# Neighbourhood attention as one stream, its transposes set one by one between score matmuls

## The chip, the cores and the metric

The kernel runs on one core of one Trainium2 chip. The metric is device time in microseconds (us), the median of a few executions. Before the change it is 2613.26 us (three runs, 2611.22 to 2614.13).

A core has five engines that run beside each other: TensorE (PE in the profile; its weight loads are shown as PEld), VectorE (DVE), ScalarE (ACT), GpSimd (POOL) and SyncE (SP). Here SP does nothing but issue the transfers between HBM and the on-chip memory. Each engine works off its own list of instructions in order; semaphores tie the lists together.

## The reference, cut to what matters

One encoder layer on two sequences, 1024 "prompt" and 256 "sample" tokens, model width 2048, all in float32. It normalises, projects to 9232 columns, runs two head groups beside each other, projects back and normalises again.

```
hn = rmsnorm(x, norm_w);  proj = hn @ w_in
att = neighbourhood_attention(q, k, v, rpb) * silu(gate)      # 8 heads of 128
mem = rmsnorm(bidirectional_mlstm(...)) * sigmoid(o) * silu(z) # 4 heads of 256
y   = rmsnorm(x + concat(att, mem) @ w_out)
```

The tokens lie on a grid 64 wide. In the attention, a query sees a window of 8 rows by 16 columns of keys (4 rows in the sample), with a learned bias for each relative place:

```
s = einsum(q_row, k_window) * scale + bias;  p = softmax(s);  out = einsum(p, v_window)
```

## The kernel before, in words

**Precision.** Every float32 product is made of three matmuls: each operand is split into a rounded high part and a low rest (`split`, lines 149 to 155: ACT writes the high part, line 151, DVE the rest, line 152), and high x high, high x low and low x high are added in PSUM. Transposes are matmuls against the identity, on the unsplit data.

**PSUM.** There are eight banks of 512 columns (`bank`, line 66): three with the tag "pr", five with the tag "a". A tile of a tag takes a bank once the instructions on an earlier tile of the tag have finished.

**Stages, in order of time.**

1. To about 1100 us: the projection of the first 768 tokens, in pairs of 128 columns (`pair_a`, line 316), as a seven-product Strassen scheme. Each of four rounds `r` loads a weight tile and makes seven products of six matmuls each (line 188), 384 columns wide, into seven banks: three "pr", four "a". What is left to do for a pair (`finish_a`, line 284) is a generator which the next pair pulls on between its products: `next(bg, None)` after the products 5, 4 and 2 of the rounds 0 to 2 (line 382). For the v columns (eight pairs), `finish_a` transposes: two transposes (line 310) to a bank, a copy by ACT (line 312), a store, six times over.
2. From about 1100 to 2110 us: the other 512 tokens' projections (line 499; v at line 580), the mLSTM and the attention. In four rounds `i`, the projections of a round are followed by `run` (line 1134, called at line 1161), which interleaves two streams with high priority: the mLSTM's units of head `i`, and the attention of the heads `2i` and `2i + 1`.
3. From about 2110 us: the output product (line 1302) and the last normalisation.

**The attention.** Per head there are five jobs: the sample (`na_sample`) and four column blocks of the prompt (`na_prompt`, `block`). A job loads v, and for each of its two halves makes the scores (three matmuls, line 617, 384 or 256 columns) in a bank, loads the bias, and makes the softmax (`na_softmax`): DVE adds the bias and takes the maximum (line 622), ACT takes the exponential with its sum (line 625), DVE inverts the sum (line 626), ACT scales (line 627). Then `na_transpose` turns each half: three transposes (two in the sample; line 634) into one bank, from which ACT writes the high part (line 636) and DVE the rest (line 637) to a tile `pt`, of which there is one buffer. Last comes the product with v (twelve matmuls in a block, line 743), and its way out. Queries and keys of a head (`nqk`) have one buffer too, and are loaded and split ahead of its blocks.

In program order, a block's stages are: all of its scores and softmaxes; a `yield`; the split of v and its transposes, in runs of three and three; a `yield`; the product. Units of a stream overlap, since `run` takes a new unit at each pass.

**What sets the order on the engines.** The kernel is recorded in program order and then put in order by a list scheduler, which takes for each engine, by priority (program order, with the streams of `run` first), what its model holds ready. It may mix projections into the attention, and does. The order on each engine is fixed when the program is built.

Of the kernel before, what the change touches and what calls it, by code (L numbers as in the profile page):

```python
# [1 line left out]

# [6 lines left out]
F32 = mybir.dt.float32  # L9
F32R = mybir.dt.float32r  # L10
AF = mybir.ActivationFunctionType
ALU = mybir.AluOpType

P = 128
D = 2048
KT = D // P
TS = 256
TP = 1024
# [20 lines left out]
def kernel(  # L39
# [244 lines left out]
    def finish_a(n1, Cn):  # L284
        nm = f"A{n1}"
        for j in range(2):
            if n1 >= NCH:
                break
            if QK0 <= n1 < OT0:
                ct = n1 - QK0 + j  # L290
                DM.dma_start(qb[ct], Cn[j][:, GA - 4 :])
                cv = pc(f"{nm}cv{j}")
                yield from conv_taps(cv, Cn[j], ct, GA - 2, 2)
                DM.dma_start(cD[ct][:, : GA - 2], cv[:, : GA - 2])
            else:
                if OT0 <= n1 < ZT0:
                    S.activation(Cn[j], Cn[j], AF.Tanh, scale=0.5)
                elif n1 >= GT0:
                    th = pc(f"{nm}th{j}")
                    S.activation(th, Cn[j], AF.Tanh, scale=0.5)  # L300
                    V.scalar_tensor_tensor(Cn[j], th, 1.0, Cn[j], op0=ALU.add, op1=ALU.mult)
                DM.dma_start(pT[n1 + j][:, 0:GA], Cn[j])
            yield
        if n1 >= NCH:
            yield
            yield
            for tt in range(GA // P):
                b = bank("a", f"{nm}v{tt}")
                for j in range(2):
                    PE.transpose(b[:, j * P : (j + 1) * P], Cn[j][:, tt * P : (tt + 1) * P], ident)  # L310
                o = wa.tile([P, 256], F32, tag="vo", name=f"{nm}vo{tt}", bufs=2)
                S.copy(o, b[:, :256])
                DM.dma_start(vD[(n1 - NCH) // 2][tt * P : (tt + 1) * P, :], o)
                yield

    def pair_a(n1, bg=iter(()), hook=None):
        nm = f"A{n1}"
        tags = ("pr", "pr", "pr", "a", "a", "a", "a")
        order = (1, 5, 6, 4, 7, 2, 3)
# [29 lines left out]
        for r in range(4):  # L349
# [12 lines left out]
            for i in order:  # L362
# [81 lines left out]

    bg = iter(())
    for i, n1 in enumerate(order):
        bg = pair_a(n1, bg, second_pools if i == len(order) - 1 else None)
# [166 lines left out]
    def na_softmax(nm, qs, ks, nkeys, h, boff):  # L614
        b = bank("a", f"{nm}s")
        for i, (a_, b_) in enumerate(((0, 0), (0, 1), (1, 0))):
            PE.matmul(b[:, :nkeys], qs(a_), ks(b_), start=i == 0, stop=i == 2)
        bt = na_tile("nbt", [P, NAK], f"{nm}bt", 2)[:, :nkeys]
        DM.dma_start(bt, rpb_tab[h, :, boff : boff + nkeys])
        st = na_tile("nst", [P, NAK], f"{nm}st", 3)[:, :nkeys]  # L620
        sm = na_tile("sm", [P, 4], f"{nm}sm", 4)
        V.tensor_tensor_reduce(
            st, b[:, :nkeys], bt, -1.0, 3.0e38, ALU.add, ALU.min, sm[:, 0:1],
        )
        S.activation(st, st, AF.Exp, bias=sm[:, 0:1], scale=-1.0, accum_out=sm[:, 2:3])
        V.reciprocal(sm[:, 3:4], sm[:, 2:3])
        S.mul(st, st, sm[:, 3:4])
        return st

    def na_transpose(nm, st, order, dst):  # L630
        b = bank("a", f"{nm}t")
        n = len(order)
        for i, c in enumerate(order):
            PE.transpose(b[:, i * P : (i + 1) * P], st[:, c * P : (c + 1) * P], ident)
        bv = b[:, : n * P].rearrange("p (k q) -> p k q", q=P)
        S.copy(dst[0], bv)
        V.tensor_tensor(dst[1], bv, f(dst[0]), op=ALU.subtract)

    def na_sample(h):
        nm = f"nas{h}"  # L640
        qk = na_tile("nqk", [P, 4, TP], f"{nm}qk", 1, F32R)[:, :, :TS]
        for i, src in enumerate((pT[QT0 + h], pT[KT0 + h])):
            raw = na_tile("nraw", [P, 512], f"{nm}r{i}", 2)[:, :TS]
            DM.dma_start(raw, src[:, TP:])
            split(qk[:, 2 * i], qk[:, 2 * i + 1], raw)
        yield
        v = na_tile("nv", [P, 2, 512], f"{nm}v", 2, F32R)
        raw = na_tile("nraw", [P, 512], f"{nm}rv", 2)[:, :TS]
        DM.dma_start(
            raw.rearrange("p (t c) -> p t c", c=P),  # L650
            vD[h // 2][TP:, (h % 2) * P : (h % 2 + 1) * P].rearrange("(t p) c -> p t c", p=P),
        )
        split(v[:, 0, :TS], v[:, 1, :TS], raw)
        st = [
            na_softmax(
                f"{nm}_{t}", lambda a_: qk[:, a_, t * P : (t + 1) * P],
                lambda b_: qk[:, 2 + b_, :], TS, h, BIAS_S + t * TS,
            )
            for t in range(2)
        ]  # L660
        yield
        pt = na_tile("npt", [P, 2, 768], f"{nm}pt", 1, F32R)
        for t in range(2):
            na_transpose(
                f"{nm}_{t}", st[t], (0, 1),
                [
                    pt[:, z, :512].rearrange("p (s q) -> p s q", s=2)[:, :, t * P : (t + 1) * P]
                    for z in range(2)
                ],
            )  # L670
        yield
        b = bank("a", f"{nm}o")
        for c in range(2):
            for i, (a_, b_) in enumerate(((0, 0), (0, 1), (1, 0))):
                PE.matmul(
                    b[:, :TS], v[:, a_, c * P : (c + 1) * P], pt[:, b_, c * TS : (c + 1) * TS],
                    start=c == 0 and i == 0, stop=c == 1 and i == 2,
                )
        o = na_tile("nst", [P, NAK], f"{nm}ot", 3)[:, :TS]
        S.copy(o, b[:, :TS])  # L680
        DM.dma_start(mixT[h][:, TP:], o)
        yield

    def na_prompt(h):
        nm = f"nap{h}"
        hd = {}

        def setup():
# [17 lines left out]
            yield  # L706

        def block(c4):
            q, k = hd["q"], hd["k"]
            n2 = f"{nm}_{c4}"  # L710
            kc = KC0[c4]
            kv = [x_.rearrange("p (r c) -> p r c", c=64) for x_ in k]
            v = na_tile("nv", [P, 2, 512], f"{n2}v", 2, F32R)
            raw = na_tile("nraw", [P, 512], f"{n2}vr", 2)
# [3 lines left out]
            st = [  # L718
                na_softmax(
                    f"{n2}_{rh}",  # L720
                    lambda a_: q[a_][:, rh * 512 + c4 * P : rh * 512 + (c4 + 1) * P],
                    lambda b_: kv[b_][:, 4 * rh : 4 * rh + 12, kc : kc + 32],
                    NAK, h, (BKIND[c4] * 2 + rh) * NAK,
                )
                for rh in range(2)
            ]
            yield
            split(v[:, 0], v[:, 1], raw)
            pt = na_tile("npt", [P, 2, 768], f"{n2}pt", 1, F32R)
            for rh in range(2):  # L730
                na_transpose(
                    f"{n2}_{rh}", st[rh], ((1, 2, 0), (0, 1, 2))[rh],
                    [
                        pt[:, z].rearrange("p (s r q) -> p s r q", r=2, q=P)[:, :, rh, :]
                        for z in range(2)
                    ],
                )
            yield
            b = bank("a", f"{n2}o")
# [7 lines left out]
            ov = hd["o"].rearrange("p (r c) -> p r c", c=64)  # L747
# [5 lines left out]
            )  # L753
            S.copy(ov[:, ng:, cs], bv[:, ng:])
            if c4 == 3:
                DM.dma_start(mixT[h][:, :TP], hd["o"])
            yield

        yield setup()
        for c4 in range(4):  # L760
            yield block(c4)

    def ml_tris():
        t = mid("tris")
# [383 lines left out]
    for i in range(ML_H):  # L1148
# [319 lines left out]
```

## Time and profile before

| | |
|---|---|
| median of three runs | 2613.26 us (2611.22 to 2614.13) |
| the profiled execution | 2613.54 us |
| its span, first to last instruction | 2611.8 us |
| instructions | 42439 |
| matmuls, transposes among them | 14470 |
| VectorE busy | 1930.9 us |
| ScalarE busy | 1311.1 us |
| bytes moved | 389.10 MB |

The profile is of one execution on the chip. A row of a group names line, engine, operation, the tiles written and read, and shapes; "x12" counts its instructions. PE rows carry the matmuls, PEld rows the loads of their weights, which run beside matmuls. In the order of time, a row gives the start, the length from the first start to the last end, and the group; neighbours of one kind are one row. The ends of matmuls are modelled, so matmuls that follow each other overlap in the record. A wait row reads: who waited, for whom, us in total, times, the longest.

The costliest groups (busy us, mean ns of one, then idle before it and who ended it):

```profile
L1302 PE MATMUL po<-wo,mo 128*128 128x512 f32 x1620 | 381.8, 396 | 12.1 <-DVE wo L152 10.2
L152 DVE TENSOR_TENSOR ws<-wr,ws 128x512 fp32r<-128x512 f32 x224 | 152.1, 694 | 93.9 <-ACT ws L151 87.9
L151 ACT CAST ws<-wr 128x512 fp32r<-128x512 f32 x224 | 136.0, 619 | 145.0 <-PE pc L499 102.4
```

The first is the output product, the others are the casts of weights in the second stage.

### The profile page before, as it was taken

What the parts mean: (1) busy time and instruction counts of PE and PEld (TensorE: products, weight loads), DVE (VectorE), ACT (ScalarE), POOL (GpSimd) and SP (SyncE); (2) the same over time, 40 slices, a digit from 0 to 9 for tenths busy, and PEclk for the clock granted to TensorE, in tenths of its full rate; (3) what the DMA queues carried; (4) which work ended last, traced back from release to release, by engine and by line L of the source; (5) the groups of instructions that cost most, each with busy time, mean ns of one, the idle gap of its engine ahead of it and who ended that gap; (6) DMA issues with size and microseconds to landing.
All of it is one profiled execution on the core that took longest, in us unless ns stands there. A gap on an engine that the chain in (4) does not pass through costs nothing.

```text
span 2611.8 us, 42439 instructions
## 1 busy us (share of the span) xinstructions
PE 2571.7 (98%) x14470; PEld 2361.3 (90%) x14470; DVE 1930.9 (74%) x3744; ACT 1311.1 (50%) x2988; POOL 706.1 (27%) x951
## 2 busy tenths in 40 slices
PE   8999999999999999999999999999999999899998
PEld 8899999999999999988998999989888888787776
DVE  7858778887878789874587587577568544889696
ACT  7534444444444444543576566576566422344445
POOL 0434444454444444300011001011001000536132
PEclk9999999999999999999999999999999999999999
DMA  6423343333333232534656556656555658446327
GB/s 207 156 77 120 102 130 112 97 99 103 95 99 110 77 117 90 164 122 147 191 161 190 185 169 189 194 163 180 180 180 172 215 174 297 140 127 197 96 81 254
DMA packets 215648, 389.10 MB, mean 149 GB/s; under 512 B 26976, under 2 KB 116232, under 8 KB 215432
## 3 DMA queue, kind: packets, MB, share of 16 engines
q1 hardware_dynamic: 215432, 386.40, 46.3%
q8 instruction: 114, 1.87, 0.3%
q14 instruction: 102, 0.84, 0.1%
HBM read 314.94 MB, written 71.38 MB: 148 GB/s over the span
## 4 chain that ended last, share of the span: by engine, by line
PE 82%; DVE 7%; DMA 6%; ACT 2%; issue 1%; POOL 1%; SPq 1%; ACTq 0%; POOLq 0%; DVEq 0%
PE pc L499 20%; PE po L1302 10%; PE pv L580 5%; DVE mo L152 1%; DVE wo L152 1%; PE A24b L188 1%; PE A16b L188 1%; PE A8b L188 1%; PE A12b L188 1%; PE A20b L188 1%; PE A52b L188 1%; PE A48b L188 1%; PE A44b L188 1%; PE A40b L188 1%; PE A70b L188 1%
## 5 line engine op out<-in xcount | busy, mean ns | idle before, releaser
L1302 PE MATMUL po<-wo,mo 128*128 128x512 f32 x1620 | 381.8, 396 | 12.1 <-DVE wo L152 10.2
L1302 PEld LDWEIGHTS po<-wo,mo 128*128 128x128 f32 x1620 | 305.3, 189 | 87.8 <-DVE wo L152 14.3
L152 DVE TENSOR_TENSOR ws<-wr,ws 128x512 fp32r<-128x512 f32 x224 | 152.1, 694 | 93.9 <-ACT ws L151 87.9
L151 ACT CAST ws<-wr 128x512 fp32r<-128x512 f32 x224 | 136.0, 619 | 145.0 <-PE pc L499 102.4
L151 ACT CAST mo<-mb 128x640 fp32r<-128x640 f32 x72 | 51.9, 725 | 110.0 <-PE po L1302 96.4
L152 DVE TENSOR_TENSOR mo<-mb,mo 128x640 fp32r<-128x640 f32 x72 | 69.1, 967 | 38.1 <-ACT mo L151 37.5
L102 POOL TENSOR_SCALAR mls_0r<-mls_0r 128x2 f32<-128x2 f32 x4 | 0.9, 237 | 248.1 <-ACT mls_0jk L1089 248.1
L1252 DVE TENSOR_TENSOR y<-y,po 128x512 f32<-128x512 f32 x90 | 57.6, 678 | 12.8 <-PE po L1302 12.8
L151 ACT CAST mo<-ms 128x640 fp32r<-128x640 f32 x40 | 29.0, 725 | 71.0 <-PE po L1302 36.2
L152 DVE TENSOR_TENSOR wsv<-wr_v,wsv 128x512 fp32r<-128x512 f32 x64 | 43.7, 690 | 22.2 <-ACT wsv L151 21.8
L1267 POOL TENSOR_TENSOR y<-y,fnb 128x512 f32<-128x512 f32 x30 | 48.9, 1649 | 38.0 <-ACT jk L1265 37.5
L151 ACT CAST wsv<-wr_v 128x512 fp32r<-128x512 f32 x64 | 39.1, 616 | 38.8 <-PE pc L499 23.1
L152 DVE TENSOR_TENSOR mo<-ms,mo 128x640 fp32r<-128x640 f32 x40 | 47.3, 1183 | 13.4 <-ACT mo L151 13.4
L165 DVE TENSOR_TENSOR pco<-pc,rstdb 128x512 f32<-128x512 f32 x48 | 32.7, 687 | 31.5 <-PE pc L499 29.8
L1229 POOL TENSOR_TENSOR wb_0a<-wb_0a,wb_0b 128x512 f32<-128x512 f32 x2 | 2.6, 1296 | 184.3 <-DVE wo L152 184.3
L1216 DVE TENSOR_TENSOR ms<-mb,mb 128x640 f32<-128x640 f32 x40 | 47.3, 1182 | 0.0
L274 DVE SCALAR_TENSOR_TENSOR pcv<-pco,cw_sb,pcv 128x516 f32<-128x516 f32 x64 | 46.7, 743 | 0.0
L1265 ACT ACTIVATE jk<-y 128x512 f32<-128x512 f32 x40 | 25.3, 631 | 40.1 <-DVE y L1252 38.6
L188 PE MATMUL fb<-xg,fw 128*128 128x384 f32 x192 | 35.1, 336 | 1.7 <-ACT xg L158 1.7
L188 PEld LDWEIGHTS fb<-xg,fw 128*128 128x128 f32 x192 | 33.3, 188 | 2.2 <-ACT xg L158 2.2
L499 PE MATMUL pc<-x_2h,ws 128*128 128x512 f32 x112 | 35.3, 398 | 0.0
L499 PE MATMUL pc<-x_0h,ws 128*128 128x512 f32 x112 | 35.2, 399 | 0.0
(1701 smaller groups left out, 8250.8 us busy)
## 6 DMA issues: line engine op xcount, KB each, us to landing
wr<-in_w_in_dram SPq DMA_DIRECT2D x112, 512.0 KB
wr_v<-in_w_in_dram SPq DMA_DIRECT2D x32, 512.0 KB
xq<-in_xtok_dram SPq DMA_DIRECT2D x20, 512.0 KB
mb<-mx SPq DMA_DIRECT2D x32, 320.0 KB
y<-in_xtok_dram SPq DMA_DIRECT2D x40, 256.0 KB
wr_wp<-in_w_o_dram SPq DMA_DIRECT2D x16, 512.0 KB
xr<-in_xT_dram SPq DMA_DIRECT2D x16, 384.0 KB
nap_0bt<-in_rpb_tab_dram SPq DMA_DIRECT2D x32, 192.0 KB
```

Source lines behind the costliest of these rows:

```text
L151: S.copy(hi, src)
L152: V.tensor_tensor(lo, src, f(hi), op=ALU.subtract)
L165: V.tensor_tensor(o, src, rb, op=ALU.mult)
L188: PE.matmul(o, w(a_), x(b_), start=first and m == 0, stop=last and m == 2)
L274: V.scalar_tensor_tensor(dst[:, a:n], src[:, a + j - pad : n + j - pad], cw_sb[:, ct, j : j + 1], dst[:, a:n], op0=ALU.mult, op1=ALU.add,)
L499: PE.matmul(pb[j], t[j][:, wi, c : c + P], xs[xi], start=first and m == 0, stop=last and m == 2,)
L580: PE.matmul(outs[tt], xs[:, tt * P : (tt + 1) * P], t[:, wi, q * w : (q + 1) * w], start=first and m == 0 and (gates or tt % 2 == 0), stop ...
L1216: V.tensor_tensor(t, x, y_, op=op)
L1252: V.tensor_tensor(Y[p, q, tt], Y[p, q, tt], bk, op=op)
L1265: S.activation(jk, Y[p, q, tt], AF.Square, accum_out=ss[t][:, c : c + 1])
L1267: G.tensor_tensor(Y[p, q, tt], Y[p, q, tt], fnb[c], op=ALU.mult)
L1302: PE.matmul(bk[tt], m[xi][:, tt * P : (tt + 1) * P], w[wi], start=first and kk == 0 and j == 0, stop=last and j == 2, skip_group_check=True,)
```

## The change

It has two parts; the arithmetic is the same.

*v transposes in `finish_a`.* Four transposes share one bank, where two did, and there is a `yield` after each of them, so that each stands behind another product of the next pair. A new flag `every` lets the pair behind a v pair pull on the generator after all seven products of the rounds 0 to 2, and not after three of them. Two copies follow the fourth transpose.

*The attention as one stream.* The jobs of both heads of a round, ten in all, become objects (`Sample`, `Block`), and one generator `na_stream` takes them through in steps. Step `t` starts the v load of job `t`, then puts the score matmuls of job `t` and the transposes of job `t - 1` in turn, one of the first, one of the second. `chained` fixes that order on PE by dependencies without semaphores; other instructions may still come between. Behind them in program order stand: the evictions of the transposes, the softmaxes of job `t` (with their bias loads), the split of v of job `t - 1`, the queries and keys for job `t + 1`, and the product of job `t - 2`. Each step is one unit for `run`.

```diff
-            for tt in range(GA // P):
-                b = bank("a", f"{nm}v{tt}")
-                for j in range(2):
-                    PE.transpose(b[:, j * P : (j + 1) * P], Cn[j][:, tt * P : (tt + 1) * P], ident)
-                o = wa.tile([P, 256], F32, tag="vo", name=f"{nm}vo{tt}", bufs=2)
-                S.copy(o, b[:, :256])
-                DM.dma_start(vD[(n1 - NCH) // 2][tt * P : (tt + 1) * P, :], o)
+            for t2 in range(GA // P // 2):
+                for _ in range((2, 4, 3)[t2]):
+                    yield
+                b = bank("a", f"{nm}v{t2}")
+                for m in range(4):
+                    tt, j = 2 * t2 + m // 2, m % 2
+                    PE.transpose(b[:, m * P : (m + 1) * P], Cn[j][:, tt * P : (tt + 1) * P], ident)
+                    if m < 3:
+                        yield
+                for tt in (2 * t2, 2 * t2 + 1):
+                    o = wa.tile([P, 256], F32, tag="vo", name=f"{nm}vo{tt}", bufs=2)
+                    S.copy(o, b[:, tt % 2 * 256 : tt % 2 * 256 + 256])
+                    DM.dma_start(vD[(n1 - NCH) // 2][tt * P : (tt + 1) * P, :], o)
                 yield
...
-                elif i in (5, 4, 2):
+                elif every or i in (5, 4, 2):
                     next(bg, None)
...
+    def chained(ops):
+        prev = None
+        for op in ops:
+            ins = op().ins
+            if prev is not None:
+                tc.add_manual_dep(ins, prev.name, NOSYNC, reason="interleave")
+            prev = ins
...
+    def na_stream(heads):
+        jobs = []
+        for h in heads:
+            hd = {}
+            jobs += [Sample(h), *(Block(h, c4, hd) for c4 in range(4))]
+        n = len(jobs)
+        st = {}
+        jobs[0].prep()
+        yield
+        for t in range(n + 2):
+            cur = jobs[t] if t < n else None
+            old = jobs[t - 1] if 0 < t <= n else None
+            smx, evs = [], []
+            if cur:
+                cur.values()
+            so, to = [], []
+            for z in range(2):
+                if old:
+                    ops, ev = old.transposed(z, st[t - 1][z])
+                    to += ops
+                    evs.append((len(to), ev))
+                if cur:
+                    ops, sm = cur.scores(z)
+                    so += ops
+                    smx.append(sm)
+            seq = []
+            for i in range(max(len(so), len(to))):
+                seq += so[i : i + 1] + to[i : i + 1]
+            chained(seq)
+            for _, ev in evs:
+                ev()
+            if cur:
+                st[t] = [sm() for sm in smx]
+            if old:
+                old.vsplit()
+            if t + 1 < n:
+                jobs[t + 1].prep()
+            if 0 <= t - 2:
+                jobs[t - 2].out()
             yield
...
-            [u for h in (2 * i, 2 * i + 1) for u in (na_sample(h), *na_prompt(h))],
+            [na_stream((2 * i, 2 * i + 1))],
```

The bodies of `scores`, `transposed`, `vsplit` and `out` are those of the functions before, cut apart.

More of the change, by code (lines that the diff above doesn't have):

```diff
@@ L1 @@
 from contextlib import ExitStack
+from functools import partial
 import concourse.bass as bass
@@ L446 @@
     for i, n1 in enumerate(order):
-        bg = pair_a(n1, bg, second_pools if i == len(order) - 1 else None)
+        bg = pair_a(
+            n1, bg, second_pools if i == len(order) - 1 else None, i > 0 and order[i - 1] >= NCH
+        )
         if i == 1:
@@ L612, in na_tile, with na_scores, mm, softmax @@
         return ap.tile(shape, dt, tag=tag, name=name, bufs=bufs)
-    def na_softmax(nm, qs, ks, nkeys, h, boff):
-        b = bank("a", f"{nm}s")
[L616 to L628, printed above, removed]
+    def chained(ops):
[5 more added lines that the diff above has]
+            prev = ins
+    def na_scores(nm, qs, ks, nkeys, h, boff):
+        b = bank("a", f"{nm}s")
+        def mm(i):
+            a_, b_ = ((0, 0), (0, 1), (1, 0))[i]
+            return PE.matmul(b[:, :nkeys], qs(a_), ks(b_), start=i == 0, stop=i == 2)
+        def softmax():
+            bt = na_tile("nbt", [P, NAK], f"{nm}bt", 2)[:, :nkeys]
+            DM.dma_start(bt, rpb_tab[h, :, boff : boff + nkeys])
+            st = na_tile("nst", [P, NAK], f"{nm}st", 3)[:, :nkeys]
+            sm = na_tile("sm", [P, 4], f"{nm}sm", 4)
+            V.tensor_tensor_reduce(
+                st, b[:, :nkeys], bt, -1.0, 3.0e38, ALU.add, ALU.min, sm[:, 0:1],
+            )
+            S.activation(st, st, AF.Exp, bias=sm[:, 0:1], scale=-1.0, accum_out=sm[:, 2:3])
+            V.reciprocal(sm[:, 3:4], sm[:, 2:3])
+            S.mul(st, st, sm[:, 3:4])
+            return st
+        return [partial(mm, i) for i in range(3)], softmax
     def na_transpose(nm, st, order, dst):
@@ L632, in na_transpose @@
         n = len(order)
[L633 to L657, printed above, removed]
-            )
[L659 to L665, printed above, removed]
@@ L670, in na_sample, with out, __init__, prep @@
             )
[L671 to L688, printed above, removed]
+        def out(self):
+            v, pt = self.v, self.pt
+            b = bank("a", f"{self.nm}o")
+            for c in range(2):
+                for i, (a_, b_) in enumerate(((0, 0), (0, 1), (1, 0))):
+                    PE.matmul(
+                        b[:, :TS], v[:, a_, c * P : (c + 1) * P], pt[:, b_, c * TS : (c + 1) * TS],
+                        start=c == 0 and i == 0, stop=c == 1 and i == 2,
+                    )
+            o = na_tile("nst", [P, NAK], f"{self.nm}ot", 3)[:, :TS]
+            S.copy(o, b[:, :TS])
+            DM.dma_start(mixT[self.h][:, TP:], o)
+    class Block:
+        def __init__(self, h, c4, hd):
+            self.h, self.c4, self.hd = h, c4, hd
+            self.nm = f"nap{h}_{c4}"
+        def prep(self):
+            if self.c4:
+                return
+            h, hd, nm = self.h, self.hd, f"nap{self.h}"
             t = na_tile("nqk", [P, 4, TP], f"{nm}qk", 1, F32R)
```

111 lines of the change are left out of this document (72 added, 39 removed).

## The prediction, made before the changed kernel was run

> **What bounds the kernel now.** I read the page's totals and slices first, then a table of three stretches, then who PE waited for, and last the order of time around single transposes.
>
> ```profile
> span 2611.8 us, 42439 instructions
> PE 2571.7 (98%) x14470; PEld 2361.3 (90%) x14470; DVE 1930.9 (74%) x3744; ACT 1311.1 (50%) x2988; POOL 706.1 (27%) x951
> ...
> PEclk9999999999999999999999999999999999999999
> ```
>
> TensorE (PE) is busy for 98% of the span, and its clock is granted in full in every slice. No other engine comes near it. The profile warns that the ends of matmuls are modelled, so "busy" alone proves little; what counts is where PE stood idle. The table of stretches gives that: length of the stretch, then busy time and instructions of each engine.
>
> ```profile
> core 0: us, PE busy (x) PEld busy (x) DVE busy (x) ACT busy (x) POOL busy (x), PEclk, DMA share, GB/s
> 90.00:1100.00 1010.00, 1010.00 (x5850) 1006.74 (x5850) 809.65 (x1441) 460.14 (x1111) 459.33 (x544) 1.00 0.33 105
> 1100.00:2110.00 1010.00, 1005.67 (x6165) 896.24 (x6164) 682.69 (x1734) 586.42 (x1395) 79.27 (x277) 1.00 0.56 177
> 2110.00:2612.00 502.00, 480.74 (x2051) 385.98 (x2049) 371.56 (x453) 196.63 (x356) 159.18 (x114) 0.99 0.51 170
> ```
>
> The first row is the projection phase of the first 768 tokens, in which the v transposes (line 310) stand: PE idles 0.00 of 1010 us. The second holds all of the attention with the mLSTM and the remaining projections: PE idles 1010.00 - 1005.67 = 4.33 us. The third is the output product, which the change doesn't touch. So the waits that the change can remove are 4.33 us in all, 0.17% of the time. Anything larger has to come out of PE's work itself. These are the waits in the second stretch (us in total, times, longest):
>
> ```profile
> PE mlp_3tp L1096 <- DVE nap_1sm L622: 1.8, 2, 1.5
> PE nap_0s L617 <- ACT mlp3a2kf L968: 0.9, 1, 0.9
> PE mlp1a2kv L921 <- POOL mlp1a0v L915: 0.8, 1, 0.8
> PE mlp2a2kv L921 <- issue: 0.5, 1, 0.5
> PE mlp_1acc L921 <- ACT mlp_1x L1054: 0.2, 1, 0.2
> ```
>
> No transpose is in this list. Line 634 (attention transposes) never waited.
>
> **What a transpose costs in a run and alone.** This decides the change, because it breaks runs. Here is a run of six between projection matmuls (start in us, length, then the group):
>
> ```profile
> 1401.85 0.49 PE L634 MATMUL nap_0t<-ident,nap_0st 128*128 128x128 f32 x3
> 1402.18 0.49 PE L634 MATMUL nap_1t<-ident,nap_1st 128*128 128x128 f32 x3
> 1402.43 1.18 PE L499 MATMUL pc<-x_4h,ws 128*128 128x512 f32 x4
> 1403.44 0.39 PE L499 MATMUL pc<-x_4l,ws 128*128 128x512 f32 x1
> 1403.67 0.39 PE L499 MATMUL pc<-x_5l,ws 128*128 128x512 f32 x1
> 1403.90 0.62 PE L499 MATMUL pc<-x_5h,ws 128*128 128x512 f32 x2
> ```
>
> Three transposes take 1402.18 - 1401.85 = 0.33, so 0.11 us each. The next matmul seems to start only 0.25 after the second three, as if the last transpose took 0.03. That is a trap: a start is recorded before the weights are in, and the matmul behind lasts longer for it. So I count over whole stretches: 1403.44 - 1401.85 = 1.59 us hold six transposes and four 512-wide matmuls at 0.23 (1403.67 - 1403.44, and again to 1403.90). (1.59 - 0.92) / 6 = 0.112 us for each.
>
> Lone transposes exist already, in the projection phase:
>
> ```profile
> 576.82 0.69 PE L188 MATMUL A20b<-xg,A20s 128*128 128x384 f32 x3
> 577.35 0.27 PE L310 MATMUL A62v<-ident,A62c 128*128 128x128 f32 x1
> 577.37 0.94 PE L188 MATMUL A20b<-xg,A20s 128*128 128x384 f32 x4
> 578.15 0.27 PE L310 MATMUL A62v<-ident,A62c 128*128 128x128 f32 x1
> 578.18 0.59 PE L188 MATMUL A20b<-xg,A20s 128*128 128x384 f32 x2
> 578.61 1.20 PE L188 MATMUL A20b<-xb,A20s 128*128 128x384 f32 x6
> 579.65 1.03 PE L188 MATMUL A20b<-xg,A20s 128*128 128x384 f32 x5
> ```
>
> Six plain 384-wide matmuls take 579.65 - 578.61 = 1.04, or 0.173 each. From 576.82 to 578.61 are 1.79 us with nine of them (1.56) and two lone transposes: 0.23 / 2 = 0.115 each. Alone or in a run, a transpose costs the same. The weight loads of those instants say why:
>
> ```profile
> 577.17 0.14 PEld L310 LDWEIGHTS A62v<-ident,A62c 128*128 128x128 f32 x1
> 577.35 0.65 PEld L188 LDWEIGHTS A20b<-xg,A20s 128*128 128x128 f32 x4
> 577.99 0.14 PEld L310 LDWEIGHTS A62v<-ident,A62c 128*128 128x128 f32 x1
> ```
>
> The load for the matmul behind the transpose begins at 577.35, the instant at which the transpose starts, not earlier. A 384-wide matmul (0.173) covers the next load; a transpose is too short to. Whatever follows it, one load of about 0.11 lies open. Interleaving hides the transpose's own load, which the matmul in front of a run hid for only one of them, but it opens the load of each score matmul behind.
>
> **The change part by part.** The instructions are the same before and after, on all engines; only their order, some PSUM banks and some waits differ. In the built order of PE, neighbouring pairs of transposes fall from 332 to 160: 143 fewer in the attention, 32 fewer among the v transposes, 3 more in the mLSTM. Runs of length one rise from 19 to 280.
>
> - *Broken runs*: 172 x (0.115 - 0.112) = +0.5 us. The rows' rounding allows 0 to 172 x 0.005 = +0.9. I take +0.5. [...]
> - *v transposes* (line 310): the same 96, now four to a bank, with 48 copies as before. PE idles 0.00 us in that phase, so nothing can be won. Behind a late copy on ACT stand the casts of the next weights; ACT is busy 460 of 1010 us, and that hides the shift. If the cover went, one such wait has been 0.3 us (row below): eight pairs x 0.3 = 2.4. I take 0.
>
> ```profile
> L310 PE MATMUL A62v<-ident,A62c x12: 270/271/272, 577.3 to 598.6; 128*128 128x128 f32 x12
> ...
>   ACT A56vo L312: 0.3, 1
> ```
>
> - *Softmax cover*: between a half block's last score and its first transpose stand now at least 40 other matmuls, before 31 (medians 101 and 101). At the stage's mean of 1005.67 / 6165 = 0.163 us that is 6.5 us against 5.1. The chain between them is, by its rows, 0.55 + 0.62 + 0.19 + 0.61 = 2.0 us and its queueing. It waited for nothing at 31, so it won't at 40.
>
> ```profile
> L622 DVE CUSTOM_DVE_ANT_0 nap_0st<-nap_0s,nap_0bt x32: 542/550/558, 1270.1 to 2039.6; 128x384 f32<-128x384 f32 x32
> L625 ACT ACTIVATE nap_0st<-nap_0st,nap_0sm x32: 600/617/652, 1272.7 to 2040.5; 128x384 f32<-128x384 f32 x32
> L625 ACT ACTIVATION_READ_ACCUMULATOR nap_0st<-nap_0st,nap_0sm x32: 183/187/227, 1273.2 to 2041.0; 128x1 f32 x32
> L627 ACT ACTIVATE nap_0st<-nap_0st,nap_0sm x32: 600/614/627, 1275.1 to 2041.5; 128x384 f32<-128x384 f32 x32
> ```
>
> - *The five waits*: for the two mlp_3tp waits (1.8) the distance in front grows from 54 to 61 and from 58 to 65 matmuls, 7 x 0.163 = 1.1 us each, so I take off 1.6. mlp2a2kv loses five (35 to 30): +0.8. mlp1a2kv gains one: -0.2. The nap_0s wait is for a bank; I leave it, since another of its kind is as likely. Sum -1.0; the ends are -4.3 (all gone) and the rival below.
> - *Waits and queues*: PE gets 21 more separate semaphore waits. The nearest row is the one below, 51 ns each: at most +1.1 us. They stand behind queued matmuls, so I take 0. The block's v loads, its bias loads and the next head's q and k loads move on SP's queue past weight loads; no wait of PE in that stretch is for a DMA, and each block's data is asked for at least as early as before, so 0. POOL's work is the same and it is busy 79 of 1010 us.
>
> ```profile
> L634 PEldq EVENT_SEMAPHORE  x22: 51/51/51, 1266.9 to 2039.5; - x22
> ```
>
> - *The end*: the last 2034 PE instructions stand in the same order, so the 21.26 us of idle after 2110 stay.
>
> Sum: +0.5 - 1.0 = -0.5 us against the profiled execution, which took 2613.54 (span 2611.8 and 1.7 around it) and lies 0.3 over the median of 2613.26. **2613 us.**
>
> **Rivals.**
>
> *A, the transposes vanish between matmuls.* The load of the matmul behind would have to run ahead of the transpose; then each broken pair would cost the 0.03 that the start times suggest, not 0.11: 172 x 0.08 = 14 us less, **2599**. For it: the start times (577.35 and 577.37). Against it: the load rows and the sums over whole stretches. [...] Here the load went one matmul ahead and no further. Chance 0.08.
>
> *B, slower: ACT stuck at the eviction of the transposes.* The tile for them (pt) has one buffer. The copy at line 636 writes it and must wait for the previous block's product (line 743). Behind it in ACT's queue stand the weight casts (line 151) on which PE lives; its banks too, of five that the mLSTM shares, stay taken. The wait exists:
>
> ```profile
> ACT nap_3pt L636 <- PE nap_2o L743: 15.9, 8, 4.3
> ```
>
> In the built order the first half's transposes stand mostly 20 to 63 matmuls ahead of that product, before mostly 9 to 32; so pt is wanted some 3 us earlier than it comes free. Today PE feels none of the 15.9 us. It decides once ACT's stop outlasts the weights already cast. If in each of the four head groups two or three stops reach PE at the 0.9 of the bank wait above, that is 10 x 0.9 = 9 us: **2622**. Against it: ACT is busy only 586 of 1010 us, so it can catch up, and bank reuse hardly tightens (under 25 matmuls in 48 of 497 cases, before 42 of 496). Chance 0.25.
>
> *C, it doesn't do what it says*: excluded by the built order, except for 19 neighbouring pairs left in the attention; its time would be the forecast's.
>
> **How the numbers follow.** Forecast, within 0.2% (5.2 us, about what a measurement can tell from none): 0.67; A 0.08; B 0.25. Low end: the median less all 4.33 us, less 1.5 for the scatter of the runs, 2607. High end: B and 1 us for the semaphore waits, 2623. Only A lies outside, and as much again beyond B.
>
> **What would show it.** Right: transposes alone between matmuls, still 0.11 to 0.12 over whole stretches; PE idle in the attention stretch 2 to 6 us; the first stretch at 0. For A: the load behind a transpose starting before it. For B: rows of PE waiting for ACT at weight casts or banks, with the ACT wait at line 636 well over 15.9. I am wrong if that idle passes 9 us or vanishes with more than 5 us gained.

## The result, and the profile after

The changed kernel takes **2629.53 us** (median of six runs, 2626.60 to 2631.16), the kernel before on the same chip 2610.46 (six runs, 2608.63 to 2614.13). The ratio is 1.0069, with a 95% interval of 1.0058 to 1.0081: slower, and 6.5 us above the top of the forecast's range. The profiled execution took 2627.55 us.

The page of the changed kernel, the same lines as before:

```profile
span 2625.5 us, 42492 instructions
PE 2577.6 (98%) x14470; PEld 2357.9 (90%) x14470; DVE 1921.5 (73%) x3744; ACT 1308.5 (50%) x2988; POOL 703.3 (27%) x951
...
PEclk9999999999999999999999999999999999999999
```

The page says almost nothing: the same work, the same clock, PE at 98%. The table of stretches of the changed kernel (columns as before) does:

```profile
90.00:1100.00 1010.00, 1004.11 (x5795) 995.64 (x5794) 791.19 (x1422) 449.22 (x1091) 457.00 (x544) 1.00 0.32 102
1100.00:2110.00 1010.00, 1002.58 (x6158) 892.36 (x6156) 684.87 (x1738) 588.58 (x1403) 78.28 (x277) 1.00 0.57 178
```

In the first row PE idles 1010.00 - 1004.11 = 5.89 us, where it was 0.00, and fits 55 matmuls fewer (5850 before) into the same 1010 us. In the second it idles 7.42, where it was 4.33. To put both kernels on one scale I cut the trace at events rather than times: the last matmul of the first v pair's own products (216.5 us before, 216.6 after; its transposes come behind it), the last matmul of the projections of the first 768 tokens, and the first of the output product. The stretch between the last two is, before and then after:

```profile
1102.60:2196.00 1093.40, 1089.07 (x6521) 963.30 (x6520) 718.00 (x1786) 606.26 (x1427) 79.27 (x277) 1.00 0.57 179
```

```profile
1112.10:2211.70 1099.60, 1091.13 (x6520) 961.59 (x6519) 720.33 (x1786) 606.84 (x1428) 78.28 (x277) 1.00 0.57 178
```

Of the 13.7 us by which the spans differ, 1112.1 - 1102.6 = 9.5 arise in the projection phase and 1099.6 - 1093.4 = 6.2 in the attention stretch. The output product, the same code, was 2.0 shorter this time; between executions it scatters from 411.7 to 418.1 us, and the start of the program by some 3 us. That scatter stands in every comparison of one profile with another below, but not in the two middle stretches.

**The projection phase.** Who PE waited for in 90 to 1100 us (before: nobody):

```profile
PE A56v L313 <- DVE A56c L167: 0.6, 1, 0.6
...
PE A70v L313 <- DVE A70c L167: 0.6, 1, 0.6
```

These are the first and last of eight rows, one for each v pair: the first v transpose waits for DVE. The order of time around one of them, first in the kernel before, PE and then DVE:

```profile
571.11 1.20 PE L188 MATMUL A20b<-xb,A20s 128*128 128x384 f32 x6
572.14 5.37 PE L188 MATMUL A20b<-xg,A20s 128*128 128x384 f32 x30
577.35 0.27 PE L310 MATMUL A62v<-ident,A62c 128*128 128x128 f32 x1
```

```profile
571.23 0.54 DVE L328 TENSOR_TENSOR A62c<-A62c,A62b 128x384 f32<-128x384 f32 x1
...
575.45 0.91 DVE L165 TENSOR_TENSOR A62c<-A62c,rstdb 128x384 f32<-128x384 f32 x1
```

PE begins the next pair (A20) at 571.11. DVE then still has to add A62's products and to scale its columns; the columns that the first transpose reads are done at 575.45 + 0.91 = 576.36, which is 5.25 us into the pair. The transpose stands behind 36 matmuls and comes at 577.35, 6.24 into the pair: 1.0 us to spare. Now the changed kernel, PE and then DVE:

```profile
574.43 1.20 PE L190 MATMUL A20b<-xb,A20s 128*128 128x384 f32 x6
575.47 2.62 PE L190 MATMUL A20b<-xg,A20s 128*128 128x384 f32 x12
577.93 0.51 PE L190 MATMUL A20b<-xb,A20s 128*128 128x384 f32 x2
578.28 0.85 PE L190 MATMUL A20b<-xg,A20s 128*128 128x384 f32 x4
579.74 0.33 PE L313 MATMUL A62v<-ident,A62c 128*128 128x128 f32 x1 [0.61 <-DVE A62c L167]
```

```profile
574.55 0.54 DVE L334 TENSOR_TENSOR A62c<-A62c,A62b 128x384 f32<-128x384 f32 x1
...
575.65 1.93 DVE L334 TENSOR_TENSOR A62c<-A62c,A62b 128x384 f32<-128x384 f32 x4
...
578.78 0.91 DVE L167 TENSOR_TENSOR A62c<-A62c,rstdb 128x384 f32<-128x384 f32 x1
```

DVE is as fast as before: 578.78 + 0.91 = 579.69, 5.26 into the pair. But the transpose now stands behind 6 + 12 + 2 + 4 = 24 matmuls. Six take 1.04, so 24 take 4 x 1.04 = 4.16. PE has to stand until 5.31: 1.15 us lost in each of eight pairs, **9.2 us**, against 9.5 measured.

The record shows only 0.61 of the 1.15 as idle in front of the transpose. The four matmuls at 578.28 last 0.85 in the model, where four starts are 4 x 0.173 = 0.69 apart: the modelled end runs 0.16 past the point at which the next could start, and so swallows 0.16 of each stop. So I measure losses from start to start. Another 0.38 lies inside the row at 575.47 (2.46 us to the next start, for twelve matmuls that take 2.08): the weight load of the seventh starts at 576.78, 0.42 us after the one before it ended, and the profile names no releaser. I take it for a wait for a bank that the additions at 575.65 free; no row shows that.

**The attention stretch.** PE's waits of 1100 to 2212 us in the changed kernel:

```profile
PE pc L507 <- ACT ws L153: 2.4, 2, 2.2
PE mlp0a2tb L1027 <- DVE nap_0sm L642: 1.4, 1, 1.4
PE mlp_1in L1002 <- ACT mlp_1x L1135: 1.3, 1, 1.3
PE mlp3a2kv L1002 <- ACT mlp3a2w L156: 1.0, 1, 1.0
PE mlp2a2kv L1002 <- issue: 0.7, 1, 0.7
PE mlp1a2tb L1027 <- DVE nap_0sm L642: 0.5, 1, 0.5
...
```

Of the five waits of before the three largest are gone (mlp_3tp, nap_0s, mlp1a2kv); others have taken their places, and none of them is at an attention transpose. All are the mLSTM's or a projection's. In most of them PE wants a bank or an operand that DVE or ACT has not got to. The longest single one, 2.2 of the 2.4 us at line 507, is another: it is for a weight that ACT casts, and ACT itself had stood for the transfer. SP's queue and then ACT in the changed kernel, and ACT at the same weight in the kernel before:

```profile
2094.53 0.33 SPq L484 DMA_DIRECT2D wr<-in_w_in_dram  x1
2095.32 7.40 SPq L1264 DMA_DIRECT2D mb<-mx  x9
2103.26 0.33 SPq L484 DMA_DIRECT2D wr<-in_w_in_dram  x1
```

```profile
2110.38 1.14 ACT L153 CAST ws<-wr 128x512 fp32r<-128x512 f32 x2 [7.60 <-DMA wr<-in_w_in_dram]
```

```profile
2094.43 1.14 ACT L151 CAST ws<-wr 128x512 fp32r<-128x512 f32 x2 [4.72 <-DMA wr<-in_w_in_dram]
```

Nine loads of the output product's input (`mb`, 320 KB each) stand between the two weight loads, and the second goes out 2103.26 - 2094.53 = 8.73 us behind the first. Its buffer was free long before: DVE was done with the older weights at 2095.63. In the kernel before, five other loads stand at this place, and the two weight loads are 2086.40 - 2081.64 = 4.76 us apart; ACT stood 4.72 us for the weight there, and PE not at all. PE's stop, 2.0 to 2.2 us, is also in the profiles of changed_again, attn_only, v_late5 and v_behind below, and one of 1.0 in tfirst; in the others none is above 0.2. Why the scheduler put the loads there, no run shows.

### The profile page after: what moved, and what is told of

The parts are those of the page before. It is cut to its first block, busy times and chain, and to the rows that moved or that the text cites. A ratio compares the mean times of both kernels' runs of the same rounds, so it can differ in the third digit from the quotient of the medians.

```text
span 2625.5 us, 42492 instructions
## 1 busy us (share of the span) xinstructions
PE 2577.6 (98%) x14470; PEld 2357.9 (90%) x14470; DVE 1921.5 (73%) x3744; ACT 1308.5 (50%) x2988; POOL 703.3 (27%) x951
## 4 chain that ended last, share of the span: by engine, by line
PE 44%; DVE 6%; DMA 5%; ACT 1%; issue 1%; SPq 1%; POOL 1%; ACTq 0%; POOLq 0%; DVEq 0%
PE pc L507 21%; PE po L1383 9%; PE pv L588 4%; DVE mo L154 1%; PE A54b L190 1%; DVE wo L154 1%; PE A52b L190 1%; DMA wr<-in_w_in_dram 1%; DVE y L1333 1%; DVE ms L1297 1%; DMA nap_0vr<-vD 1%; PE nap_0s L635 1%; PE nap_1s L635 1%; PE mlp_2in L1002 0%; SPq L755 0%
## 5 line engine op out<-in xcount | busy, mean ns | idle before, releaser
L154 DVE TENSOR_TENSOR mo<-mb,mo 128x640 fp32r<-128x640 f32 x72 | 72.2, 1010 | 39.4 <-ACT mo L153 39.2
L154 DVE TENSOR_TENSOR wsv<-wr_v,wsv 128x512 fp32r<-128x512 f32 x64 | 43.9, 697 | 16.3 <-ACT wsv L153 15.7
```

The lines of the kernel that those rows point to most:

```text
L154: V.tensor_tensor(lo, src, f(hi), op=ALU.subtract)
```

## The experiments

Each kernel ran against the kernel before on the same chip, 5 to 12 runs of it beside 21 to 28 of before (the first comparison, "changed", six beside six; before_again is a single run). "+9.9 us" is always the difference of the two medians. The ratio behind it is worked out from all the runs and can differ from the ratio of the medians, by up to 0.0007 here. For orientation, all of them with the lengths of the two middle stretches in their profiles and PE's idle in the second (us):

| kernel | to before | projection | attention | idle |
|---|---|---|---|---|
| before | | 886.0 | 1093.4 | 4.3 |
| changed | +19.1 | 895.5 | 1099.6 | 8.5 |
| changed_again | +16.8 | 895.4 | 1097.9 | 7.8 |
| v_only | +9.9 | 895.3 | 1095.2 | 4.6 |
| v_only3 | -1.1 | 887.1 | 1091.4 | 3.2 |
| v_only5 | +4.7 | 887.1 | 1093.5 | 3.7 |
| v_late5 | +6.7 | 886.9 | 1101.3 | 9.1 |
| attn_only | +3.0 | 886.0 | 1098.0 | 8.0 |
| grouped | +0.9 | 885.9 | 1093.9 | 4.9 |
| halves | +7.2 | 885.9 | 1098.8 | 6.5 |
| unchained | +5.1 | 885.9 | 1098.3 | 5.4 |
| tfirst | +11.0 | 885.9 | 1105.7 | 11.3 |
| both_fixed | +2.3 | 887.3 | 1094.6 | 5.3 |
| v_behind | +2.5 | 885.9 | 1094.1 | 3.5 |
| all_behind | +8.5 | 887.1 | 1097.3 | 7.2 |

**v_only: the v transposes of the change alone.** `finish_a`, `every` and the call as changed; the attention as before.

> The kernel before with the v transposes of the change alone. Theory 1 (bank): the first transpose of a v pair now stands behind the third product, takes the spare fifth bank that the next pair's product 4 had, so product 6 waits for a bank of the pair before (0.38 us) and the transpose for the scaled columns (0.77 us): eight pairs x 1.15 = +9.2 us over the kernel before, all of it before 1112 us. Theory 2 (lone transposes cost more than runs): 32 broken pairs spread over the phase, +0.5 to +9 us with no wait at the start of the pair. If the change's loss is all in the attention: +0.

2622.05 us, **+9.9** (ratio 1.0033, 1.0022 to 1.0045). The eight waits at line 313 are there, and the phase is 895.3 us long, where it was 886.0.

**attn_only: the attention stream alone.** The v transposes as before.

> The changed kernel with the v transposes as before, so the attention stream alone. Theory 1: the loss of the first phase (9.2 us) is gone, the one of the attention stretch stays (6.2 us there in the profiles: 4.1 idle, 2.1 busy): +6 us over the kernel before, up to +10 if the medians' 19 us are to be explained. Theory 2: nearly all stays, since 140 of the 172 broken pairs are here: +15. If the v part is all of the loss: +0.

2615.18 us, **+3.0** (1.0015, 1.0006 to 1.0024); the attention stretch is 1098.0 us long, with 8.0 of idle. So the larger part of the loss lies in the part of the change that I had put at nothing.

**v_late5: the changed kernel, the first v transpose later.**

```diff
-                for _ in range((2, 4, 3)[t2]):
+                for _ in range((5, 3, 1)[t2]):
```

> The changed kernel with the first v transpose three products later, behind the sixth product as before the change; the transposes still stand one by one. Theory 1: the built order gives product 4 the spare bank again, the 1.15 us per pair go, and it is 9 us faster than the changed kernel, equal to the attention stream alone. Theory 2: the transposes are still alone, so the loss of that phase stays and it equals the changed kernel within 2 us.

2618.88 us, **+6.7** (1.0027, 1.0016 to 1.0038). The first transpose stands behind 36 matmuls again, the eight waits are gone (two of 0.3 us for ACT's copy are in their place), and the phase is 886.9 us long. I had expected it to equal attn_only; its attention stretch was 1101.3 us long, 3.3 more than there.

**grouped: the attention stream alone, all scores of a step ahead of all its transposes.**

```diff
-            seq = []
-            for i in range(max(len(so), len(to))):
-                seq += so[i : i + 1] + to[i : i + 1]
-            chained(seq)
+            chained(so + to)
```

> The attention stream with the v transposes as before, its score matmuls and transposes chained in groups (all scores of a step, then its transposes in a run), not one by one. Theory 1 (a lone transpose costs about what one in a run costs): within 2 us of the attention stream alone, +4 to +8 over the kernel before, because the stream's order and its waits stay. Theory 2 (lone transposes cost more): back to the kernel before, +0, busy time of the attention stretch 2 us lower and its idle unchanged. Rival B of the prediction (transposed tile evicted late): the same as theory 1, with the eviction's wait for the product before still grown.

2613.05 us, **+0.9** (1.0004, 0.9993 to 1.0015); stretch 1093.9, idle 4.9, as before. The time is that of the second theory, its sign is not: that theory wanted busy time to fall by 2 us and idle to stay, and against attn_only busy time fell by 0.9 (1090.0 to 1089.1) and idle by 3.1.

**changed_again: the changed kernel once more**, on the chip of the next three.

> The changed kernel once more, beside the others of this call. By the parts measured so far (v transposes +9.9, attention stream +3.0) it should be +13 us over the kernel before; the first comparison gave +19. If it is again at +19, the parts don't add and something is made by both together.

2628.92 us, **+16.8** (1.0068, 1.0055 to 1.0081).

**v_only3 and v_only5: v_only, with the first transpose one product later, and three.** `(3, 4, 2)` and `(5, 3, 1)` in place of `(2, 4, 3)`.

> The v transposes alone, their first one product later than in the change (behind the fourth). Theory 1, sharpened: the transpose needs columns that VectorE finishes 5.4 us after the pair's first matmul, and PE has only 24 matmuls (4.2 us) ahead of it; with 30 ahead (5.2 us) about 0.2 to 0.3 us are left to wait, so 8 x 0.25 = +2 us over the kernel before and the wait row at the transposes falls from 0.6 to about 0.2. Theory 2 (lone transposes cost more): no change from the v transposes alone, +9.

> The v transposes alone, their first behind the sixth product as before the change, one by one from there. Theory 1: no wait, +0 to +1 us over the kernel before, the phase to 1102 us as long as before (886 us from 216 us on). Theory 2: +5 to +9, since 24 pairs of transposes are still broken.

v_only3: 2611.00 us, **-1.1** (1.0003, 0.9994 to 1.0012). v_only5: 2616.84, **+4.7** (1.0020, 1.0011 to 1.0029). The order of time of v_only3:

```profile
571.45 1.20 PE L188 MATMUL A20b<-xb,A20s 128*128 128x384 f32 x6
572.48 3.28 PE L188 MATMUL A20b<-xg,A20s 128*128 128x384 f32 x18
575.60 0.51 PE L188 MATMUL A20b<-xb,A20s 128*128 128x384 f32 x2
575.95 0.86 PE L188 MATMUL A20b<-xg,A20s 128*128 128x384 f32 x4
576.76 0.33 PE L311 MATMUL A62v<-ident,A62c 128*128 128x128 f32 x1
...
578.68 0.27 PE L311 MATMUL A62v<-ident,A62c 128*128 128x128 f32 x1
578.71 0.60 PE L188 MATMUL A20b<-xg,A20s 128*128 128x384 f32 x2
579.14 0.27 PE L311 MATMUL A62v<-ident,A62c 128*128 128x128 f32 x1
579.17 1.30 PE L188 MATMUL A20b<-xg,A20s 128*128 128x384 f32 x6
580.30 0.27 PE L311 MATMUL A62v<-ident,A62c 128*128 128x128 f32 x1
```

The transpose comes at 576.76 - 571.45 = 5.31 us into the pair, to the hundredth the time at which it came in the changed kernel. There PE had made 24 matmuls and stood; here it has made 30. One product of six matmuls is the whole difference, and it takes 8.2 us off the phase (895.3 to 887.1). The record shows no idle in it any more; but 30 matmuls take 5 x 1.04 = 5.20, so PE still stands 0.11 in each pair, 0.9 us in all, of the 1.1 by which the phase is longer than before. In v_only5 that phase is 887.1 too, with two waits for ACT's copy (0.4 and 0.3). That is 1.1 of its 4.7 us; where the rest arises, its profile doesn't show (its attention stretch is as long as before; its output product was the longest seen, 418.1). That is left open.

**halves: attn_only with scores and transposes in runs of three.** `chained(so[:3] + to[:k] + so[3:] + to[k:])`, with `k = len(to) // 2`.

> The attention stream with the v transposes as before, chained as three scores, three transposes, three scores, three transposes: runs stay, but scores and transposes of a step still alternate by halves. If the order one by one makes the stream's loss (a step's two score banks and two transposed banks are all open at once from its second pair on), this is close to the grouped one, +0 to +2 us over the kernel before, idle of PE in the attention stretch 4 to 6 us. If it is the alternation of score and transpose as such, it is like the attention stream alone, +3, idle about 8.

2619.36 us, **+7.2** (1.0028, 1.0019 to 1.0037); stretch 1098.8, idle 6.5. Transposes in runs, as before, and no faster than one by one: the runs are not what matters. My expectation of +0 to +2, from the banks held open, missed.

**unchained and tfirst: attn_only with the order left to the scheduler, and with the transposes first.** `for op in so + to: op()`, and `chained(to + so)`.

> The attention stream with the v transposes as before and no chain at all (scores ahead of transposes in program order, the scheduler free). Theory 1: like the grouped one, within 2 us of the kernel before, PE idle of the attention stretch 4 to 5 us. If the ordering edges as such cost (they keep PE from taking what is ready), it is faster than the grouped one.

> As the grouped one, but a step's transposes chained ahead of its scores. Transposes then hold their banks while the scores still need theirs, and the next softmax starts later. Theory 1 (what costs is scores that come late, behind transposes, with the banks open longer): +3 to +8 us over the kernel before, idle of the attention stretch 6 to 9 us. If only the alternation costs: within 2 us of the grouped one.

unchained: 2617.97 us, **+5.1** (1.0018, 1.0010 to 1.0027), stretch 1098.3. tfirst: 2623.78, **+11.0** (1.0040, 1.0028 to 1.0053), stretch 1105.7 with 11.3 of idle, more than I expected. Of these chained orders, the later the scores come in a step, the longer the stretch: 1093.9 with the scores first, 1098.0 and 1098.8 with both mixed, 1105.7 with them last. It is no rule: two kernels below break it (v_behind mixes them, at 1094.1, and all_behind has the scores first, at 1097.3). That unchained is as slow as attn_only, and not as fast as grouped, I had not expected.

**both_fixed: the changed kernel with `(3, 4, 2)` and `chained(so + to)`.**

> The changed kernel with its two loss-makers taken back, the rest kept: the first v transpose one product later, and a step's scores chained ahead of its transposes. Theory 1 (the loss is the v transposes' wait, 9.4 us, and the alternation of scores and transposes, 5 to 8 us): +0 to +2 us over the kernel before, 887 us for the first phase and about 1094 for the attention stretch. If one stream instead of units costs by itself, +4 or more.

2615.15 us, **+2.3** (1.0008, 0.9999 to 1.0017); phase 887.3, stretch 1094.6. Two edits that move no work to another engine take some 14 of the 16.8 us away again.

**before_again: the kernel before, once more**, for the scatter between profiles.

> The kernel before once more, for a second profile: its phases should be 886 us, 1093 to 1094 us, and the head and the tail, whose code is the same in all of these kernels, may scatter by 2 to 3 us each as they do among the others.

2613.58 us in one execution. Its stretches are 885.8 and 1094.3, with 0.0 and 5.0 us of idle (before: 886.0 and 1093.4, 0.0 and 4.3). These two hold within 1 us from one execution to another.

**v_behind: what the attention part waits for.** In the profile of attn_only I followed one of the waits back. ACT, DVE and PE, each in its order:

```profile
1271.26 0.62 ACT L153 CAST nap_0v<-nap_0vr 128x512 fp32r<-128x512 f32 x1 [2.51 <-DMA nap_0vr<-vD]
```

```profile
1271.91 0.69 DVE L154 TENSOR_TENSOR nap_0v<-nap_0vr,nap_0v 128x512 fp32r<-128x512 f32 x1 [2.37 <-ACT nap_0v L153]
1272.52 0.55 DVE L636 CUSTOM_DVE_ANT_0 nap_0st<-nap_0s,nap_0bt 128x384 f32<-128x384 f32 x1
```

```profile
1273.13 0.66 PE L1021 MATMUL mlp0a2tb<-ident,mlp0a2cv 128*128 128x128 f32 x4 [1.06 <-DVE nap_0sm L636]
```

ACT stands 2.51 us for the block's v to arrive, DVE 2.37 for ACT's half of the split; behind it on DVE stands the bias and maximum (line 636) that reads the scores' bank, and PE stands 1.06 for that bank. In the kernel before the same load is late by as much, and ACT (2.56 us) and DVE (1.41) stand for it too, but the two instructions of line 622 come first:

```profile
1270.08 0.55 DVE L622 CUSTOM_DVE_ANT_0 nap_0st<-nap_0s,nap_0bt 128x384 f32<-128x384 f32 x1
...
1270.62 0.54 DVE L622 CUSTOM_DVE_ANT_0 nap_1st<-nap_1s,nap_1bt 128x384 f32<-128x384 f32 x1
...
1272.58 0.69 DVE L152 TENSOR_TENSOR nap_0v<-nap_0vr,nap_0v 128x512 fp32r<-128x512 f32 x1 [1.41 <-ACT nap_0v L151]
```

In the built order of attn_only DVE's half of a v split stands ahead of its own block's bias and maximum in 15 of 80 cases, among them the first block of three of the four rounds (both halves) and one half of it in the fourth; in tfirst in 16, in grouped in 13 (of the first blocks mostly one half), before in 10. The count alone doesn't explain the times: unchained has the same 13 as grouped, and a stretch 4.4 us longer. v_behind forbids it:

```diff
+    def vsplit_behind(nm, hi, lo, src):
+        S.copy(hi, src)
+        sub = V.tensor_tensor(lo, src, f(hi), op=ALU.subtract).ins
+        for z in range(2):
+            tc.add_manual_dep(sub, reds[f"{nm}_{z}"].name, NOSYNC, reason="behind")
```

(`reds` holds the bias-and-maximum instruction of each half; `vsplit` calls this in place of `split`.)

> The attention stream alone (v transposes as before), with one edit: on DVE the second half of the split of a job's v may not be placed ahead of the job's own two bias-and-maximum instructions. In the stream as changed the built order has it ahead of 15 of the 80, before of 10, and in the profile of the stream alone DVE stood 2.4 us for the cast of v, which stood 2.5 us for v's load, while the bank of the scores stayed taken and PE waited 1.1 us for it. Theory: this is what the attention part costs. Then PE's waits behind the bias-and-maximum go (2 of 1.1 us), the idle of the attention stretch falls from 8.0 to about 5 or 6 us, and the time to before +0 to +1.5 us, from +3.0. Rival: the cost lies in how scores and transposes alternate, whatever DVE does in between. Then it stays at +3 us and 8 us of idle, with other names in the waits.

2613.97 us, **+2.5** (1.0011, 1.0002 to 1.0020). In its profile the waits behind the bias and maximum are gone, and the stretch is 1094.1 us long, about as long as before, with 3.5 of idle, of which 2.0 are the stop for the weight load:

```profile
1103.70:2197.80 1094.10, 1090.59 (x6521) 962.69 (x6520) 719.71 (x1785) 607.32 (x1428) 81.71 (x277) 1.00 0.57 179
```

The profile says what the theory said, a stretch 3.9 us shorter than in attn_only; the medians, 3.0 against 2.5, can't tell it from the rival. The scatter of single runs (2609 to 2618) is as large as what is sought.

**all_behind: both_fixed with the same edit.**

> The changed kernel with three edits: the first v transpose one product later, all scores of a step ahead of its transposes, and the split of v behind the job's own bias-and-maximum on DVE. With the first two alone it was 2.3 us over before, with 5.3 us of idle in the attention stretch, where 13 of 80 bias-and-maximum instructions still stood behind a split of v. If the late split is what is left: before -1 to +1 us, idle 3 to 5. If not: +2.3 as it was.

2620.03 us, **+8.5** (1.0026, 1.0017 to 1.0035): a clear miss. Its stretch is 1097.3 us long with 7.2 of idle, and PE's waits are others again:

```profile
PE nap_0s L643 <- ACT mlp1a2kf L1054: 1.6, 1, 1.6
PE mlp_1in L1007 <- ACT mlp_1x L1140: 1.5, 1, 1.5
...
```

One dependency more, and the scheduler lays out the whole stream in another way. In the attention stretch, then, the late split accounts for the waits that name it, and forbidding it is not a lever by itself: the orders tried have between 3.5 and 11.3 us of PE idle in this stretch, each at other places.

## Why the prediction was wrong

- **v transposes, put at 0: this step failed.** I argued that "PE idles 0.00 us in that phase, so nothing can be won", looked for the risk at the copy behind the transposes, on ACT, and priced the loss of its cover at 8 x 0.3 = 2.4. The loss was ahead of them, on DVE: 8 x 1.15 = 9.2 us. Both numbers stood in the trace of before: DVE done 5.25 us into the pair, the transpose 6.24 into it, 1.0 us or not quite six matmuls to spare. The built order showed the transpose moved twelve matmuls forward, 2.1 us. 2.1 - 1.0 = 1.1 us for each pair could have been worked out blind. v_only shows that the part costs it, v_only3 that six matmuls in front take nearly all of it away (8.2 us of the phase). The copy, where I had looked, shows as 0.6 us of PE's idle in v_late5 and 0.7 in v_only5, and as none in the changed kernel.
- **Broken runs, +0.5: right in kind.** In v_only3, 580.30 - 579.14 = 1.16 us hold one transpose and six matmuls at 0.173: 0.12 for the transpose; 579.14 - 578.68 = 0.46 hold one and two: 0.11. In the attention stretch PE's busy time is 1090.0 us in attn_only, where all stand alone, and 1089.1 in grouped, where they stand in runs, before 1089.1. So 143 broken runs cost at most about 1 us, if the stops that the record hides in busy time are alike in both.
- **Rival A is out** by the same numbers: nothing vanished.
- **Softmax cover, 0: right.** No row of PE's waits in the changed kernel is at an attention transpose (line 658).
- **The five waits, -1.0: wrong in sign.** The sum has a slip besides: of mlp_3tp's two waits the longest was 1.5 and so the other 0.3, and a distance of 1.1 us takes off 1.1 + 0.3 = 1.4, not 1.6; the term would be -0.8, and the forecast 2613 still. The three largest went; but new ones of the same kind came, and idle in the stretch rose from 4.3 to 8.5 us. I took the list of waits as what there is to win. It was what this one order had left over.
- **Loads on SP's queue, 0: failed too, in two places.** v is asked for as early as before (1264.74 us in attn_only, 1265.58 before) and waited for as long (2.5 us). What changed is who stands behind the wait: the instruction that frees the scores' bank. And I set only the attention's loads against the weights. The output product's, nine in a row, now stand ahead of a weight load, and PE stands 2.2 us for it, the longest of its waits in the stretch. I asked when a load goes out, and not what is queued behind its arrival, nor what else is queued ahead of a weight.
- **Rival B: its mechanism is out.** ACT's waits of the transposes' eviction for the product fell from 25.2 to 15.4 us; the row quoted in the prediction (15.9 us) has become the first of these:

```profile
ACT nap_3pt L662 <- PE nap_2o L788: 7.0, 4, 2.3
ACT nap_1pt L662 <- PE nap_0o L788: 6.5, 5, 2.1
```

No row shows PE waiting for line 662. The sign that it named, PE waiting for ACT at a weight cast, is there (2.2 us), but ACT stood for the weight's transfer, 42 us after the last eviction of transposes. Its other half, that scores and transposes hold banks which the mLSTM needs, is what the rows of mlp0a2tb and mlp1a2tb behind nap_0sm (1.4 and 0.5 us) show, by way of DVE. With two buffers for `pt` (the run pt2) the kernel gave no result: their pool needs 117.97 kB of each partition, and 113.75 are left. So what the single buffer costs is not shown by a run.
- **The end, 0**: right within its scatter.

What stays open: the two parts alone come to 9.9 + 3.0 = 12.9 us, the whole to 16.8 and 19.1. The intervals (about 3 us on each) leave a difference of 0 to 10; the two middle stretches give 9.5 + 6.2 = 15.7. Open too are v_only5's 4.7 us, and why unchained differs from grouped.

No version beats the kernel before; v_only3 (1.0003), grouped (1.0004) and both_fixed (1.0008, 0.9999 to 1.0017) can't be told from it.

## What to carry to other kernels

Where an instruction is moved forward on the bound engine, take from the trace when its operand is ready and when it is reached, both counted from the same point; the difference, in matmuls, is how far it may move, and a stretch without idle says nothing about how near the edge it is (here 0.00 us of idle, with 1.0 us to spare). Of a wait that isn't new, ask again what stands behind it in the new order. And where a scheduler lays out the stream, a list of small waits is a property of one order: removing them one by one bought others of the same size here (the three largest gone, and idle from 4.3 to 8.5 us).

## What was not expected of the hardware

A stop of PE is recorded too short by some 0.16 us, since the modelled end of a 384-wide matmul runs that far past its turn (0.85 for four that take 0.69): 5.89 us of recorded idle stood for 9.5 lost. And the same instructions, in the output product, took 411.7 to 418.1 us in different executions, at a granted clock of 0.99 to 1.00 (from 2212 to 2600 us); the middle stretches of the kernel before held within 1 us between two executions (886.0 and 885.8, 1093.4 and 1094.3).
